# Where the split activations and weights begin within a partition: one offset mod 256 for all of them

## The chip, the cores and the metric

The kernel runs on one core of a Trainium2 chip. The metric is the device time of one execution in microseconds. The kernel before takes 2351.78 us, the median of 3 runs that lie between 2351.42 and 2352.85 us.

## What is computed

One inference step of a hybrid backbone, one layer, for 128 context tokens and 256 latent tokens (384 in all), with 2048 channels, in float32. Nearly all of the work is dense products of the 384 tokens with large weight matrices:

```python
mod = silu(cond) @ w_ada + b_ada                       # 2048 x 12288, two conditions
h   = rmsnorm(x) * (1 + sc1) + sh1
z   = h @ w_in + b_in                                  # 2048 x 11792
y_a, y_b, y_c = conv(z) @ w_a_out, pool(z) @ w_pool, mlstm(z) @ w_c_out
x   = x + g1 * rmsnorm((ga*y_a + gb*y_b + gc*y_c) @ w_out)   # 2048 x 2048
h2  = rmsnorm(x) * (1 + sc2) + sh2
u, g = split(h2 @ w_ffn_up)                            # 2048 x 11264
x   = x + g2 * rmsnorm((gelu(dwconv3(g)) * u) @ w_ffn_down)  # 5632 x 2048
```

The outputs are the new context and latent tokens and the final mLSTM states.

## The kernel before, in words

**Three products for one.** Every float32 operand of a large product is split into a high part, rounded to float32r, and a low part, the rest. `split` (line 163) makes them: ScalarE copies the source into the high tile (line 164), VectorE subtracts it from the source (line 165). `mm3` (line 172) then issues three float32r matmuls into one PSUM bank: high weight with high activation (line 173), high weight with low activation (line 174), low weight with high activation (line 175). The profile names them by output, then stationary and moving operand: `ps<-hx,whi` multiplies an activation tile `hx` with a weight tile `whi`.

**The stream.** The weights pass through a list of pieces (`run_stream`, line 183), each up to 128 x 1024 floats (512 KB). SyncE loads a piece into one of four `raw` tiles, `split` makes `whi` and `wlo` of it (three tiles of each), two pieces ahead of the matmuls that use it. While a piece is in use, functions of other work (`bgq`) are issued behind it. The order of pieces is fixed by the program. In the first stage there are separate tiles `eraw`, `ehi`, `elo` for `w_ada`.

**The stages.** In order of time: the modulation and the first tiles of `w_in` (to about 155 us of the span); the rest of the input projection with the mLSTM heads beside it (to about 560 us); the merge gates with the three branch projections (to about 1080 us); `w_out` (to about 1204 us); the second norm and `w_up` (to about 1970 us); the 88 pieces of `w_down` (to the end).

- In the input projection, merge gates and `w_out` stages, an `mm3` has a 128 x 128 block of weights as stationary operand and all 384 tokens of one `hx` tile as moving operand: 384 columns. A column tile of the output takes 16 `hx` tiles, `hx0` to `hx15`, 48 matmuls in all, in two pieces of 24.
- The branch projections (`ab_use`, `c_use`) do the same from the tiles `yah`/`yal` (convolution), `plh`/`pll` (pooling) and `hch`/`hcl` (mLSTM) in place of `hx`.
- In the `w_up` stage two more columns (the shift of the modulation, `H2`) hang on the tokens: 386 columns (`HW`, line 26).
- For the mLSTM values (`v_use`, line 887) and for `w_down` (`down_mm`, line 1509) the roles are exchanged: a 128-token slice of an `hx` tile is the stationary operand, the weights are the moving one, with 256 and 512 columns. In the down projection the activations are split into `hx0`, `hx1` and `hx2` in turn (`down_split`, line 1502), each used for 18 matmuls of one piece.

**Where the tiles lie.** Tiles of the three pools `cp`, `wp` and `hp` are placed one behind the other in each partition, from the left, each start rounded up to 32 bytes. Offsets here are byte offsets in the partition, taken mod 256, read from the built program. All tiles `raw`, `whi` and `wlo` are 4096 bytes long and begin at 96. The tile `hx0` begins at 96 too. An `hx` tile holds the high row and then the low row (`h_pair`, line 358). With 386 columns a row has 1544 bytes and a tile 3088, which is placed as 3104, so `hx1` begins at 128, `hx2` at 160, and so on by 32, round to 96 again at `hx8`; the low row of each begins 8 further on. With 384 columns in the down projection a row has 1536 bytes, and high and low row begin at the same offset. The branch tiles (`yah`, `yal`, `plh`, `pll`, `hch`, `hcl`), which lie behind `hx15`, all begin at 96. All slices that are taken of these tiles as matmul operands are whole multiples of 512 bytes apart, so an operand has the offset of its row. The tiles `eraw`, `ehi`, `elo` and the first stage's stationary operand `cs4` are placed from the right side and begin at 224.

So the two operands of a float32r matmul begin at the same offset in the products with `w_ada`, in the branch projections, for `hx0` in the down projection and for the high rows of `hx0` and `hx8` elsewhere, and at different ones in the rest.

Of the kernel before, what the change touches and what calls it, by code (L numbers as in the profile page):

```python
# [12 lines left out]
F32 = mybir.dt.float32  # L13
F32R = mybir.dt.float32r
# [5 lines left out]
P = 128  # L20
# [3 lines left out]
LAT = 256  # L24
NT = SEQ + LAT
HW = NT + 2
GRID_W = 64
ROWS = LAT // GRID_W
WA = 512
# [10 lines left out]

CBUF = HALF + (SEQ + HALF) + ROWS * (GRID_W + HALF)
CPOS = CBUF - 2 * HALF
CLAT0 = HALF + SEQ + HALF
CROW = GRID_W + HALF

# [47 lines left out]
def body(ctx: ExitStack, tc: tile.TileContext, i, o):  # L93
    nc = tc.nc
# [10 lines left out]
    cp = ctx.enter_context(tc.tile_pool(name="const", bufs=1, side="left"))  # L105
    wp = ctx.enter_context(tc.tile_pool(name="wp", bufs=1, side="left"))
    hp = ctx.enter_context(tc.tile_pool(name="hp", bufs=1, side="left"))
# [5 lines left out]
    def name(base):  # L113
        uid[0] += 1
        return f"{base}{uid[0]}"
# [14 lines left out]
    def tmp(tag="t", n=NT, bufs=4, dt=F32):  # L130
        return cp.tile([P, n], dt, name=name(tag), tag=tag, bufs=bufs)
# [15 lines left out]
    G2 = cp.tile([P, 2, KD], F32, name="G2")  # L147
    dp = ctx.enter_context(tc.tile_pool(name="dp", bufs=1, space=bass.MemoryType.DRAM))
    G2D = dp.tile([2, D], F32, name="G2D")

    act.dma_start(condT, i["condT"])
    act.dma_start(vec, i["vec"])
# [10 lines left out]
    def split(hi, lo, src):  # L163
        act.activation(hi, src, AF.Copy)  # L164
        dve.tensor_sub(lo, src, hi.bitcast(F32))  # L165
# [6 lines left out]
    def mm3(out, wh, wl, x, xl, first, last):  # L172
        pe.matmul(out, wh, x, start=first, stop=False, skip_group_check=True)  # L173
        pe.matmul(out, wh, xl, start=False, stop=False, skip_group_check=True)  # L174
        pe.matmul(out, wl, x, start=False, stop=last, skip_group_check=True)  # L175
# [177 lines left out]
    hx = [None] * KD  # L353
# [3 lines left out]

    def h_pair(tag, n):

        t = hp.tile([P, 2, n], F32R, name=name("hx"), tag=tag)  # L360
        pr = Two()
        pr.hi, pr.lo = t[:, 0], t[:, 1]
        return pr

    def make_h(k):

        st = {}

        def p1():
            st["t"] = tmp()  # L370
            dve.tensor_mul(st["t"], x1[:, k], R["r1"])

        def p2():
            t = st["t"]
            act.activation(t[:, :SEQ], t[:, :SEQ], AF.Identity, bias=H1[:, k, 0:1], scale=S1[:, k, 0:1])
            act.activation(t[:, SEQ:], t[:, SEQ:], AF.Identity, bias=H1[:, k, 1:2], scale=S1[:, k, 1:2])
            pr = h_pair(f"hx{k}", HW)
            pr.hi, pr.lo = pr.hi[:, :NT], pr.lo[:, :NT]
            act.activation(pr.hi, t, AF.Copy)
            hx[k] = pr  # L380

        def p3():
            dve.tensor_sub(hx[k].lo, st["t"], hx[k].hi.bitcast(F32))

        return p1, p2, p3
# [297 lines left out]
    def za_after(c):  # L683
        def f():
# [3 lines left out]
            dve.scalar_tensor_tensor(b[:, HALF : HALF + SEQ], ps[:, :SEQ], bias, s[:, :SEQ], ALU.add, ALU.mult)  # L688
            lat = b[:, CLAT0:].rearrange("p (r c) -> p r c", c=CROW)[:, :, :GRID_W]
            dve.scalar_tensor_tensor(lat, ps[:, SEQ:NT].rearrange("p (r c) -> p r c", c=GRID_W), bias,  # L690
                                     s[:, SEQ:].rearrange("p (r c) -> p r c", c=GRID_W), ALU.add, ALU.mult)
            glu["b", c] = b
# [514 lines left out]
    def scaled(out, src, G, k):  # L1207
        act.activation(out[:, :SEQ], src[:, :SEQ], AF.Copy, scale=G[:, k, 0:1])
        act.activation(out[:, SEQ:NT], src[:, SEQ:NT], AF.Copy, scale=G[:, k, 1:2])
# [19 lines left out]
    def split_mix(k):  # L1229
        pr = h_pair(f"hx{k}", HW)  # L1230
        split(pr.hi[:, :NT], pr.lo[:, :NT], mix[k])
        pr.hi, pr.lo = pr.hi[:, :NT], pr.lo[:, :NT]
        mixp[k] = pr
# [75 lines left out]
    def h2_b(k):  # L1309
        if k < KD:  # L1310
            x = X["x"][:, k]
            u = tmp("sig", HW, bufs=3)
            scaled(u, x, S2, k)
            act.activation(u[:, NT:], H2[:, k], AF.Copy)
            pr = h_pair(f"hx{k}", HW)
            act.activation(pr.hi, u, AF.Copy)  # L1316
            hx[k] = pr
            HU[k] = u
            if k == 0:
                act.activation(ss3, x, AF.Square)  # L1320
            else:
                HU["s", k] = tmp()
                act.activation(HU["s", k], x, AF.Square)
# [7 lines left out]
    def h2_step(k):  # L1331
        h2_a(k + 1)
        h2_b(k)
        h2_c(k)
# [20 lines left out]
    def up0_use(k):  # L1355
        def f(hi, lo):
            for c in range(NUP0):
                if k == 0:
                    acc["up", c] = accbank() if c < 2 else bank(2 + c)
                w = slice(c * P, (c + 1) * P)  # L1360
                mm3(acc["up", c][:, :HW], hi[:, w], lo[:, w], hx[k].hi, hx[k].lo, k == 0, k == KD - 1)
            h2_step(k + 2)
# [8 lines left out]
    def up_after(n):  # L1371
# [5 lines left out]
        def first():  # L1377
            pu, pg = acc[("up", 2 * n)], acc[("up", 2 * n + 1)]
            r = R["r3"]
            hb = tmp("hb", 4, bufs=2)  # L1380
            act.activation(hb[:, 0:2], pu[:, NT:HW], AF.Copy)
            act.activation(hb[:, 2:4], pg[:, NT:HW], AF.Copy)
# [100 lines left out]
    def g2_rows():  # L1483
# [4 lines left out]
        act.activation(row[0 : 2 * KD], ps[0 : 2 * KD, 0:P], AF.Copy)  # L1488
        gp.dma_start(G2D.rearrange("c (k p) -> (c k) p", p=P), row[0 : 2 * KD])
        g2_load(0)  # L1490

    def g2_load(h):
        t = F["p"].tile([P, 2, HALF_D], F32, name=name("gb"), tag="gb")
        for c in range(2):
            gp.dma_start(t[:, c], G2D[c : c + 1, HALF_D * h : HALF_D * (h + 1)].broadcast_to([P, HALF_D]))
        DN["g", h] = t
# [209 lines left out]
```

## Time and profile before

| | |
|---|---|
| time, median of 3 runs | 2351.78 us |
| time of the profiled execution | 2352.14 us |
| its span | 2350.4 us |
| granted TensorE clock, mean | 0.995 |
| PE busy | 2312.1 us (98%) |
| PEld busy | 2189.8 us (93%) |
| DVE busy | 1490.0 us (63%) |
| ACT busy | 933.8 us (40%) |
| chain of work that ended last, PE's share | 94% |

The span is the profiled execution from its first instruction to its last; the execution's own time is 1.7 us longer. PE is TensorE's matmuls, PEld its weight loads, DVE VectorE, ACT ScalarE, POOL GpSimd. Matmuls overlap: one begins before the one ahead has ended, so that the duration of one says less than the distance from its start to the next one's start, which is the time that a matmul takes of the stream. The text calls this distance the spacing. It is got from the timeline view, which gives every start to 0.01 us, as the time between two starts over the number of matmuls between them, or from the windows view as the length of a window that is full of matmuls over their number.

### The profile page before, as it was taken

To read this page: it belongs to the slowest core of one execution; us is meant where nothing else is said; L and a number is where in the kernel's file an instruction comes from. 1 tells how busy PE (TensorE), PEld (TensorE's weight loads), DVE (VectorE), ACT (ScalarE), POOL (GpSimd) and SP (SyncE) were. 2 spreads that over 40 slices of the span, in tenths; PEclk is the share of its full clock that TensorE was granted. 3 is DMA by queue.
4 is the path that set the end of the run, shared out by engine and by line. 5 is a ranking of instruction groups with operands and counts; after the bars stand their busy time and mean duration, and the time that the engine had idled before them with its cause. 6 is when DMAs were issued, how large, how long until landed. Compare 5 with 4: busy or idle time off the path is not lost.

```text
span 2350.4 us, 32026 instructions
## 1 busy us (share of the span) xinstructions
PE 2312.1 (98%) x12597; PEld 2189.8 (93%) x12597; DVE 1490.0 (63%) x2286; ACT 933.8 (40%) x1417; POOL 33.0 (1%) x72
## 2 busy tenths in 40 slices
PE   7999999999999999999999999999999999999997
PEld 3899999999999999999999999999999999888886
DVE  6876777646788777868556577776444445444444
ACT  6853333434322232324356533333333334334333
POOL 0000000000000000000000000000000000000000
PEclk9999999999999999999999999999999999999999
DMA  9954334234566666667533355554343333334332
GB/s 342 326 159 143 100 119 128 95 112 156 193 219 222 223 219 231 229 201 276 190 90 126 122 186 186 187 182 160 126 144 123 121 125 126 126 125 144 128 127 103
DMA packets 109335, 390.07 MB, mean 166 GB/s; under 512 B 12608, under 2 KB 12880, under 8 KB 109184
## 3 DMA queue, kind: packets, MB, share of 16 engines
q1 hardware_dynamic: 103968, 371.77, 47.6%
q0 software_dynamic: 4064, 14.36, 2.1%
q8 instruction: 98, 1.61, 0.3%
q10 hardware_dynamic: 1152, 1.90, 0.2%
q14 instruction: 53, 0.43, 0.1%
HBM read 382.71 MB, written 5.27 MB: 165 GB/s over the span
## 4 chain that ended last, share of the span: by engine, by line
PE 94%; DVE 2%; ACT 1%; DMA 1%; issue 1%; DVEq 0%; ACTq 0%; SPq 0%
PE ps L175 24%; PE ps L174 24%; PE ps L173 24%; PE ps L1513 5%; PE ps L1514 5%; PE ps L1512 5%; PE ps L897 1%; PE ps L899 1%; PE ps L898 1%; PE ps L400 1%; PE ps L994 1%; PE ps L989 1%; PE ps L401 1%; DMA eraw<-w_ada 0%; ACT ehi L164 0%
## 5 line engine op out<-in xcount | busy, mean ns | idle before, releaser
L165 DVE TENSOR_TENSOR wlo<-raw,whi 128x1024 fp32r<-128x1024 f32 (+2 forms) x520 | 622.5, 1199 | 755.0 <-ACT whi L164 754.8
L164 ACT ACTIVATE whi<-raw 128x1024 fp32r<-128x1024 f32 (+2 forms) x520 | 540.2, 1040 | 1272.3 <-PE ps L174 804.5
L173 PE MATMUL ps<-hx,whi 128*128 128x384 f32 (+1 forms) x3024 | 1026.7, 340 | 3.2 <-ACT hx L1316 3.2
L175 PE MATMUL ps<-hx,wlo 128*128 128x384 f32 (+1 forms) x3024 | 1026.6, 339 | 2.1 <-DVE wlo L165 2.1
L174 PE MATMUL ps<-hx,whi 128*128 128x384 f32 (+1 forms) x3024 | 1026.8, 340 | 0.1
L173 PEld LDWEIGHTS ps<-hx,whi 128*128 128x128 f32 x3024 | 571.5, 189 | 4.5 <-ACT hx L1316 3.4
L175 PEld LDWEIGHTS ps<-hx,wlo 128*128 128x128 f32 x3024 | 572.3, 189 | 3.5 <-DVE wlo L165 3.4
L174 PEld LDWEIGHTS ps<-hx,whi 128*128 128x128 f32 x3024 | 570.5, 189 | 1.8 <-DVE hx L165 0.4
L1177 DVE SCALAR_TENSOR_TENSOR cb<-raw,cb 128x1024 f32<-128x1024 f32 x256 | 313.1, 1223 | 9.2 <-DMA raw<-w_ada 3.3
L1513 PE MATMUL ps<-whi,hx 128*128 128x512 f32 x528 | 208.0, 394 | 0.8 <-DVE hx L165 0.8
L1514 PE MATMUL ps<-wlo,hx 128*128 128x512 f32 x528 | 208.2, 394 | 0.0
L1512 PE MATMUL ps<-whi,hx 128*128 128x512 f32 x528 | 207.8, 394 | 0.0
L1513 PEld LDWEIGHTS ps<-whi,hx 128*128 128x128 f32 x528 | 99.2, 188 | 24.4 <-DVE hx L165 1.1
L1512 PEld LDWEIGHTS ps<-whi,hx 128*128 128x128 f32 x528 | 99.2, 188 | 23.3 <-ACT hx L164 0.4
L1514 PEld LDWEIGHTS ps<-wlo,hx 128*128 128x128 f32 x528 | 99.2, 188 | 22.9
L165 DVE TENSOR_TENSOR elo<-eraw,ehi 128x1024 fp32r<-128x1024 f32 x56 | 66.9, 1221 | 22.8 <-ACT ehi L164 22.7
L712 DVE SCALAR_TENSOR_TENSOR cacc<-cbuf,vec,cacc 128x444 f32<-128x444 f32 x116 | 78.7, 679 | 2.8
L1404 DVE SCALAR_TENSOR_TENSOR t<-t,vec,t 128x192 f32<-128x192 f32 (+1 forms) x176 | 63.8, 383 | 16.1 <-ACT t L1395 12.9
L164 ACT ACTIVATE ehi<-eraw 128x1024 fp32r<-128x1024 f32 x56 | 56.3, 1047 | 18.8 <-DMA eraw<-w_ada 9.8
L897 PE MATMUL ps<-whi,hx 128*128 128x256 f32 x192 | 56.1, 292 | 0.0
L400 PE MATMUL ps<-ehi,cs 128*128 128x512 f32 x112 | 47.3, 422 | 6.9 <-ACT ehi L164 6.9
L898 PE MATMUL ps<-whi,hx 128*128 128x256 f32 x192 | 53.8, 280 | 0.0
(291 smaller groups left out, 1633.6 us busy)
## 6 DMA issues: line engine op xcount, KB each, us to landing
raw<-w_in SPq DMA_DIRECT2D x168, 512.0 KB, 3.9
raw<-w_up SPq DMA_DIRECT2D x164, 512.0 KB, 3.6
raw<-w_ada SPq DMA_DIRECT2D x128, 512.0 KB, 4.2
raw<-w_down SPq DMA_DIRECT2D x88, 512.0 KB, 3.2
eraw<-w_ada SPq DMA_DIRECT2D x64, 512.0 KB, 6.0
raw<-w_out SPq DMA_DIRECT2D x32, 512.0 KB, 4.6
raw<-w_v SPq DMA_DIRECT2D x16, 512.0 KB, 3.9
raw<-w_br SPq DMA_DIRECT2D x16, 512.0 KB, 4.9
```

Of the source, the lines that this page charges most:

```text
L164: act.activation(hi, src, AF.Copy)
L165: dve.tensor_sub(lo, src, hi.bitcast(F32))
L173: pe.matmul(out, wh, x, start=first, stop=False, skip_group_check=True)
L174: pe.matmul(out, wh, xl, start=False, stop=False, skip_group_check=True)
L175: pe.matmul(out, wl, x, start=False, stop=last, skip_group_check=True)
L712: dve.scalar_tensor_tensor(a, b[:, j : j + CPOS], w, a, ALU.mult, ALU.add)
L897: pe.matmul(outs[t], xh, hi[:, a], start=k == 0 and t != 1, stop=False, skip_group_check=True)
L898: pe.matmul(outs[t], xl, hi[:, a], start=False, stop=False, skip_group_check=True)
L1177: dve.scalar_tensor_tensor(MX["junk"], raw, 1.0, MX["cb"][c][half], ALU.mult, ALU.mult, accum_out=MODR[:, m, n, c, half : half + 1])
L1512: pe.matmul(ps, xh, hi[:, w], start=first, stop=False, skip_group_check=True)
L1513: pe.matmul(ps, xl, hi[:, w], start=False, stop=False, skip_group_check=True)
L1514: pe.matmul(ps, xh, lo[:, w], start=False, stop=last, skip_group_check=True)
```

## The change

The offsets are made equal, by four edits. An `hx` tile gets two rows of 448 floats (1792 bytes, 7 times 256), whatever the number of columns in use, so a tile has 3584 bytes (14 times 256) and both rows of all sixteen tiles begin at one offset. A tile `spare` of 128 bytes that nothing uses is put into the first pool, which moves all tiles behind it by 128: `raw`, `whi`, `wlo`, all `hx` rows and the branch tiles now begin at 224, where the tiles placed from the right side begin. The longer `hx` tiles need 7680 bytes more; for them the scratch area for the descriptors of GpSimd's DMAs, at the start of each partition, is halved from 16384 to 8192 bytes (itself a multiple of 256).

```diff
+HPITCH = 448
...
+    cp.tile([P, 32], F32, name="spare")
...
     def h_pair(tag, n):
 
-        t = hp.tile([P, 2, n], F32R, name=name("hx"), tag=tag)
+        t = hp.tile([P, 2, HPITCH], F32R, name=name("hx"), tag=tag)
         pr = Two()
-        pr.hi, pr.lo = t[:, 0], t[:, 1]
+        pr.hi, pr.lo = t[:, 0, :n], t[:, 1, :n]
         return pr
...
-    nc = bacc.Bacc("TRN2", target_bir_lowering=False, num_devices=1)
+    nc = bacc.Bacc("TRN2", target_bir_lowering=False, num_devices=1, dynamic_dma_scratch_size=8192)
```

The instructions of every engine and queue are the same as before in kind, shape and order; only addresses differ, and line numbers behind the first edits by 1 to 3.

## Rows read from the trace of the kernel before

**Rows 1.** The page: busy time of each engine; chain that ended last, by engine.
```profile
PE 2312.1 (98%) x12597; PEld 2189.8 (93%) x12597; DVE 1490.0 (63%) x2286; ACT 933.8 (40%) x1417; POOL 33.0 (1%) x72
PE 94%; DVE 2%; ACT 1%; DMA 1%; issue 1%; DVEq 0%; ACTq 0%; SPq 0%
```

**Rows 2.** Groups by line and form: count, busy us, mean ns, idle before.
```profile
L174 PE MATMUL ps<-hx,whi 128*128 128x384 f32 x1616 | 545.9, 338 | 0.1
...
L174 PE MATMUL ps<-hx,whi 128*128 128x386 f32 x1408 | 481.0, 342 | 0.0
...
L1513 PE MATMUL ps<-whi,hx 128*128 128x512 f32 x528 | 208.0, 394 | 0.8 <-DVE hx L165 0.8
...
L898 PE MATMUL ps<-whi,hx 128*128 128x256 f32 x192 | 53.8, 280 | 0.0
```

**Rows 3.** Waits, all engines: who for whom, us in total, times, longest.
```profile
ACT whi L164 <- PE ps L174: 804.5, 329, 5.7
...
PE ps L175 <- DVE wlo L165: 2.1, 4, 0.6
```

**Rows 4.** Windows, all instructions: the stages, PE count in brackets, clock, DMA share.
```profile
0.00:155.00 155.00, 136.68 (x610) 102.37 (x611) 109.06 (x147) 106.19 (x150) 7.24 (x15) 0.98 0.83 296
...
155.00:560.00 405.00, 404.04 (x2444) 388.50 (x2443) 273.52 (x513) 154.78 (x234) 16.83 (x40) 1.00 0.37 116
560.00:1080.00 520.00, 518.98 (x2957) 518.01 (x2956) 405.68 (x582) 169.36 (x205) 6.30 (x12) 1.00 0.66 219
1080.00:1195.00 115.00, 115.00 (x655) 115.00 (x654) 72.48 (x96) 41.68 (x66) 0.00 (x0) 1.00 0.60 202
```

**Rows 5.** Windows, instructions on `hx` tiles alone: first stage, up projection, down projection.
```profile
0.00:155.00 155.00, 52.11 (x288) 50.54 (x289) 8.76 (x16) 8.42 (x16) 0.98 0.83 296
...
1400.00:1900.00 500.00, 500.00 (x2818) 499.84 (x2818) 0.00 (x0) 0.00 (x0) 1.00 0.47 153
2050.00:2300.00 250.00, 250.00 (x1081) 202.77 (x1080) 33.15 (x60) 30.46 (x60) 1.00 0.40 130
```

**Rows 6.** Timeline of PE, a branch projection: start us, duration us, instruction.
```profile
580.12 0.33 PE L173 MATMUL ps<-yah,whi 128*128 128x384 f32 x1
...
580.82 0.35 PE L174 MATMUL ps<-yal,whi 128*128 128x384 f32 x1
...
582.22 0.33 PE L173 MATMUL ps<-plh,whi 128*128 128x384 f32 x1
...
582.74 0.33 PE L173 MATMUL ps<-hch,whi 128*128 128x384 f32 x1
...
586.90 0.33 PE L173 MATMUL ps<-hx,whi 128*128 128x384 f32 x1
```

**Rows 7.** Durations, ns, min/median/max: `hch` matmuls; line 174, 1400 to 1900 us.
```profile
L173 PE MATMUL ps<-hch,whi x128: 334/334/334, 582.7 to 1067.8; 128*128 128x384 f32 x128
...
L174 PE MATMUL ps<-hx,whi x939: 336/341/347, 1400.2 to 1899.8; 128*128 128x386 f32 x188
```

**Rows 8.** Timeline of PE, down projection: `hx2` from 2203.82, `hx0` from 2208.01, `hx1` from 2212.13.
```profile
2203.82 0.40 PE L1512 MATMUL ps<-whi,hx 128*128 128x512 f32 x1
...
2208.01 0.39 PE L1512 MATMUL ps<-whi,hx 128*128 128x512 f32 x1
...
2209.86 0.39 PE L1514 MATMUL ps<-wlo,hx 128*128 128x512 f32 x1
...
2211.90 0.40 PE L1514 MATMUL ps<-wlo,hx 128*128 128x512 f32 x1
2212.13 0.39 PE L1512 MATMUL ps<-whi,hx 128*128 128x512 f32 x1
```

**Rows 9.** Timeline of PE, mLSTM values, two rows 51 matmuls apart.
```profile
185.92 0.28 PE L897 MATMUL ps<-whi,hx 128*128 128x256 f32 x1
...
191.92 0.28 PE L897 MATMUL ps<-whi,hx 128*128 128x256 f32 x1
```

**Rows 10.** GpSimd's own load: the tokens for the second norm, issue, first use, landing.
```profile
L1297 DVE TENSOR_TENSOR x<-mo,x x16: 557/558/560, 1209.3 to 1253.9; 128x384 f32<-128x384 f32 x16
...
L1222 POOL DMA_DIRECT2D x<-xT x4: 527/528/530, 1064.6 to 1066.2; - x4
...
DMA to landing us min/median/max: 7.1/9.7/13.6
```

## The prediction

> **What bounds the kernel now.** First the page's busy times and its chain: PE is busy for 98% of the span and has 94% of the chain that ended last [rows 1]. Next the waits, to see whether something else sets PE's pace. They run the other way: ScalarE waited 804.5 us in all for PE to give weight tiles back, and PE's matmuls of line 175 waited 2.1 us for VectorE's low part [rows 3]. The granted clock is 1.00 in every stage from 155 us on, so 2.4 GHz [rows 4]. So from 155 us to the end the time is the number of matmuls times their spacing, and a change that only moves addresses can only act through that spacing, or not at all. In the first 155 us PE is not full (136.68 us, 610 matmuls, DMA share 0.83) [rows 4].
>
> So the question for the trace is whether the spacing depends on where operands begin. It does. The matmuls on `hch` have equal offsets for both operands. From the first of them at 582.74 us to the first `hx` matmul at 586.90 us there are 24: 4.16 us, **173.3 ns** each [rows 6]. In the `w_out` stage the same shape comes from `hx` tiles at eight offsets: 655 matmuls in 115.00 us, **175.6 ns** [rows 4]. The durations say the same: 334 ns for all 128 `hch` matmuls of a line, without any spread, and 336 to 347 ns among the `hx` matmuls of 386 columns [rows 7]. The down projection is the cleanest case, since there only the offset of the tile differs from one piece to the next: the 18 matmuls on `hx2` take 4.19 us (2203.82 to 2208.01), 232.8 ns each; the 18 on `hx0`, where the offsets are equal, 4.12 us (to 2212.13), 228.9 ns; and within these, once it has settled, 9 matmuls take 2.04 us (2209.86 to 2211.90), **226.7 ns** [rows 8]. It takes some matmuls to settle: the 12 on `yah`/`yal`, equal in offset but behind a run of unequal ones, take 2.10 us (580.12 to 582.22), 175.0 ns each, one of them 0.35 us long, and then the 3 on `plh` run at 173.3 [rows 6].
>
> I read this as two streams of reads, the moving operand and the next weights, that get in each other's way for a few ns per matmul unless they run in step, and as a state in step that a run of equal offsets finds and keeps. The change puts all of the stream into it.
>
> **A rule against it.** The Trainium skill, TensorE: Matmul & The Clock Gate, "Step-by-step: what each phase is for", says that PE has two independent SBUF read ports, so that "Loading the next tile's weights doesn't steal SBUF read bandwidth from the running matmul." By that rule offsets would not matter and the change would give nothing; the rows above, 228.9 against 232.8 ns for one shape in neighbouring pieces, do not agree with it. It stays as a rival below.
>
> **The terms.** No instruction is added, removed or moved on any engine or queue. What is left is the spacing, form by form, with counts from the groups (three lines per form) [rows 2].
>
> - *384 columns on `hx`.* 3 x 1616 = 4848, of which 288 lie in the first 155 us [rows 5], where PE has slack; I count 4560. They go from 175.6 to 173.3: 4560 x 2.3 ns = 10.5 us. The branch projections are in step already; only the settling of `yah` goes, 192 matmuls x 1.7 ns = 0.3 us.
> - *386 columns.* 3 x 1408 = 4224. Now 2818 matmuls take 500.00 us, 177.4 ns [rows 5]. No row shows this form in step. Between 384 and 512 columns the spacing in step grows by 53.4 ns for 128 columns, 0.417 ns a column, so two columns more would give 173.3 + 0.8 = 174.1. That is one end, and the value I take, because the same slope holds between two forms that were seen and the start of both reads is what the state in step seems to hang on. 4224 x 3.3 ns = 13.9 us. The other end is above today's spacing: a row of 1544 bytes does not end on a multiple of 256, unlike 1536 and 2048, so the step could be lost at each row's end. A duration is 334 - 173.3 = 161 ns longer than its spacing, so the longest seen in this stage, 347 ns [rows 7], is a spacing of 186: 4224 x 8.6 = 36 us of loss.
> - *512 columns.* 3 x 528 = 1584, now 1081 in 250.00 us, 231.3 ns [rows 5], in step 226.7: 1584 x 4.6 = 7.3 us.
> - *256 columns.* 3 x 192 = 576, now 51 in 6.00 us, 117.6 ns [rows 9]. By the slope in step it would be 226.7 - 256 x 0.417 = 119.9, so here being in step costs: 576 x 2.3 = 1.3 us. The other end is no change.
> - *What is behind PE.* With 1.3% less time for PE, every split must be 1.3% sooner. VectorE is busy 405.68 of 520 us in the merge stage and the DMA share is 0.66 [rows 4], so both stay below PE. In the input projection the head work comes in bursts, and some weights will be later than PE wants them; I give back 1 us. At nothing I take the splits themselves (ScalarE and VectorE read and write the same tiles at equal offsets before and after) and the halved scratch area: of GpSimd's DMAs the ones with a due time are the tokens for the second norm, issued from 1064.6 us, landed within 13.6, and first used at 1209.3 [rows 10]. If that cover of 130 us were not enough, PE would wait at 1209 us.
>
> Sum: 10.5 + 0.3 + 13.9 + 7.3 - 1.3 - 1.0 = 29.7 us. Against the profiled execution's 2352.1 us that is 2322.4; the median of the runs is 0.3 lower, so I forecast **2322 us** (1.3% faster). A measurement of this kernel can tell about 0.2% (4.7 us) from no change.
>
> **The rivals.**
>
> 1. *386 columns find no step.* The state in step holds for rows that are multiples of 256 bytes and not for 1544. For it: no aligned run of 386 columns was ever seen. Against it: with unequal offsets the 386 form stands above the 384 form by only 177.4 - 175.6 = 1.8 ns, so its odd end seems to cost little. The term of 13.9 us falls away: 2336 us, and up to 2347 if the spacing rises to 180.
> 2. *386 columns collide each time (slower).* Equal starts with rows that end 8 bytes past a multiple of 256 might bring the two reads together at the same place in every matmul, where unequal ones spread it. Place: the `w_up` stage, 1211 to 1970 us. It decides from the spacing at which it eats the other terms, 15.8 us / 4224 = 3.7 ns above today's 177.4, so from 181.1 ns on; at 186, 36.3 us of loss against 15.8 of gain, 2372 us. Such a spacing is among those seen [rows 7], but as the worst of a mixture whose mean is 177.4.
> 3. *The offsets do nothing.* The 173.3 ns of `hch` comes from something else about the branch tiles (high and low rows lie far apart there), and the two reads never meet: 2352 us. Against it stands `hx0` beside `hx1` and `hx2`, which are alike but for their offset [rows 8]. The rule of the Trainium skill named above (TensorE: Matmul & The Clock Gate) speaks for this rival.
> 4. *The gain is lost in waits.* PE's shorter pieces run into late splits or loads in the input projection and merge stages, so only the up and down projections gain: 13.9 + 7.3 = 21 us, 2331; if it holds everywhere, 2340 or more. Against it: 804.5 us of ScalarE waiting for PE [rows 3].
>
> **How the numbers follow.** The forecast 0.72; rival 1, 0.13; rival 2, 0.05; rival 3, 0.05; rival 4, 0.05. The forecast's own range is 2317 (nothing lost at 256 columns or in waits, and some `hx` runs better still) to 2330 (386 columns at 176, a bit of waiting). With most of rivals 1 and 4 the range is 2316 to 2340. Faster by over 0.2%: the forecast, rival 1 and most of rival 4, 0.89; within 0.2%: rival 3, 0.05; slower: rival 2 with a little for mishaps, 0.06.
>
> **What the profile after should show.** Durations of 334 ns without spread for 384-column matmuls on `hx`, as on `hch` now, and near 388 for 512 columns. In the windows, 1400 to 1900 us: about 2870 matmuls if 386 columns run at 174.1, 2818 or fewer if rival 1 or 2 holds. In the down projection pieces of 18 matmuls that all take 4.08 us, whichever `hx` tile. The counts of instructions unchanged. The prediction is wrong if `hx` matmuls of 384 columns keep a spread of durations; the theory stands but its size is off if only the 386-column stage does.

## The result: 19.3 us faster, and the profile after

The changed kernel takes 2332.68 us (median of 4 executions, 2331.24 to 2332.71) beside 2351.97 us before (median of 4, 2351.42 to 2352.85). The ratio is 0.9916, 95% interval 0.9904 to 0.9928: 19.3 us less. The forecast was 2322 us. The profiled execution shown here took 2332.71 us, with a span of 2330.9 us.

The page, first the busy times of the engines, then the chain of work that ended last (compare [rows 1]):

```profile
PE 2292.1 (98%) x12597; PEld 2177.4 (93%) x12597; DVE 1490.2 (64%) x2286; ACT 934.0 (40%) x1417; POOL 33.1 (1%) x72
...
PE 94%; DVE 2%; DMA 2%; ACT 1%; issue 1%; DVEq 0%; ACTq 0%; SPq 0%
```

PE still bounds the kernel, with the same counts of instructions; it is busy for 20.0 us less, which covers the whole change. The groups by form (line, engine, form and count, then busy us, mean ns, idle before) answer to [rows 2]; all line numbers are larger by 3. In these names the moving operand stands first and the stationary one second, and not the other way round as was said ahead of the prediction: `hx,whi` are 384 or 386 columns of activations that move, with a block of weights stationary, and `whi,hx` is the reverse.

```profile
L177 PE MATMUL ps<-hx,whi 128*128 128x384 f32 x1616 | 540.2, 334 | 0.2 <-DVE hx L168 0.2
...
L177 PE MATMUL ps<-hx,whi 128*128 128x386 f32 x1408 | 477.9, 339 | 0.0
...
L1516 PE MATMUL ps<-whi,hx 128*128 128x512 f32 x528 | 205.5, 389 | 0.8 <-DVE hx L168 0.8
...
L901 PE MATMUL ps<-whi,hx 128*128 128x256 f32 x192 | 54.3, 283 | 0.0
```

The mean duration of the 384-column matmuls fell from 338 to 334 ns and that of the 512-column ones from 394 to 389; the 386-column ones fell by only 3 ns, from 342 to 339, and stand 5 ns above the 384-column ones for two columns more. The durations of single forms (min/median/max in ns, with the first and the last start) say more than their means:

```profile
L177 PE MATMUL ps<-hx,whi x944: 338/339/342, 1400.0 to 1899.9; 128*128 128x386 f32 x189
...
L1516 PE MATMUL ps<-whi,hx x368: 389/389/389, 2049.9 to 2299.5; 128*128 128x512 f32 x184
```

In `w_out`, line 177 has 334/334/334 ns, as the `hch` matmuls had before [rows 7]. The down projection has lost its spread too. The up projection has kept one. The windows, of instructions on `hx` tiles alone (columns: length; busy us with count of PE, PEld, DVE, ACT; granted clock, DMA share, GB/s), answer to [rows 5]:

```profile
1400.00:1900.00 500.00, 500.00 (x2831) 499.84 (x2830) 0.00 (x0) 0.00 (x0) 1.00 0.46 153
2050.00:2300.00 250.00, 250.00 (x1105) 207.01 (x1104) 34.14 (x62) 30.87 (x61) 1.00 0.40 131
```

2831 matmuls of 386 columns in 500 us are 176.6 ns each (before, 177.4); 1105 of 512 columns in 250 us are 226.2 (before, 231.3). A window also counts the matmuls that are cut by its ends, so these run 0.1 to 0.5 ns low. From here on "mean spacing" is the mean of all distances from one matmul's start to the next one's in a stage, without the gaps; the records give starts to 1 ns. The timeline of PE (start us, duration us, instruction) shows three places: the start of the up projection, its middle, and one piece of the down projection.

```profile
1201.96 0.69 PE L176 MATMUL ps<-hx,whi 128*128 128x386 f32 x1 [3.24 <-ACT hx L1319]
...
1203.05 0.53 PE L178 MATMUL ps<-hx,wlo 128*128 128x386 f32 x1
...
1207.87 0.36 PE L178 MATMUL ps<-hx,wlo 128*128 128x386 f32 x1
...
1499.95 0.34 PE L176 MATMUL ps<-hx,whi 128*128 128x386 f32 x1
1500.13 0.34 PE L177 MATMUL ps<-hx,whi 128*128 128x386 f32 x1
1500.30 0.34 PE L178 MATMUL ps<-hx,wlo 128*128 128x386 f32 x1
1500.48 0.34 PE L176 MATMUL ps<-hx,whi 128*128 128x386 f32 x1
...
2208.11 0.39 PE L1515 MATMUL ps<-whi,hx 128*128 128x512 f32 x1
...
2212.18 0.39 PE L1515 MATMUL ps<-whi,hx 128*128 128x512 f32 x1
```

The 18 matmuls of the piece at 2208.11 take 4.07 us; before, they took 4.12 on `hx0` and 4.19 on `hx2` [rows 8]. In the middle of the up projection the starts do not come evenly: by the records, spacings of 175 and 178 ns alternate.

Where the 19.4 us between the two spans come from, by the first matmul of each stage in the two traces:

| stage | gained there, us | gained up to its end, us |
|---|---|---|
| first stage and first part of the input projection, to the mLSTM values | 0.8 | 0.8 |
| rest of the input projection | 1.5 | 2.3 |
| merge gates and branch projections | 5.6 | 7.9 |
| `w_out` and the second norm | 1.6 | 9.5 |
| up projection | 2.4 | 11.9 |
| down projection | 7.7 | 19.6 |

The end of the kernel behind the last of these matmuls gives about 0.15 us back.

### The profile page after: what moved, and what is told of

It is laid out like the page before. It is cut to its first block, busy times and chain, and to the rows that moved or that the text cites. A ratio compares the mean times of both kernels' runs of the same rounds, so it can differ in the third digit from the quotient of the medians.

```text
span 2330.9 us, 32026 instructions
## 1 busy us (share of the span) xinstructions
PE 2292.1 (98%) x12597; PEld 2177.4 (93%) x12597; DVE 1490.2 (64%) x2286; ACT 934.0 (40%) x1417; POOL 33.1 (1%) x72
## 4 chain that ended last, share of the span: by engine, by line
PE 94%; DVE 2%; DMA 2%; ACT 1%; issue 1%; DVEq 0%; ACTq 0%; SPq 0%
PE ps L177 24%; PE ps L178 24%; PE ps L176 24%; PE ps L1516 5%; PE ps L1515 5%; PE ps L1517 5%; DMA eraw<-w_ada 1%; PE ps L901 1%; PE ps L902 1%; PE ps L900 1%; PE ps L997 1%; PE ps L992 1%; PE ps L403 0%; DVE wlo L168 0%; PE ps L404 0%
## 5 line engine op out<-in xcount | busy, mean ns | idle before, releaser
L167 ACT ACTIVATE whi<-raw 128x1024 fp32r<-128x1024 f32 (+2 forms) x520 | 540.3, 1040 | 1252.7 <-PE ps L177 773.6
L1516 PE MATMUL ps<-whi,hx 128*128 128x512 f32 x528 | 205.5, 389 | 0.8 <-DVE hx L168 0.8
L1515 PE MATMUL ps<-whi,hx 128*128 128x512 f32 x528 | 205.5, 389 | 0.0
L902 PE MATMUL ps<-wlo,hx 128*128 128x256 f32 x192 | 54.3, 283 | 0.0
```

The source lines that it names most:

```text
L1515: pe.matmul(ps, xh, hi[:, w], start=first, stop=False, skip_group_check=True)
L1516: pe.matmul(ps, xl, hi[:, w], start=False, stop=False, skip_group_check=True)
```

## The experiments

"Distance" is the offset of an activation row less that of the weights it meets, mod 256. The kernel before ran beside the experiments at 2352.67 us (median of 7; `no_spare`, `up392`, `up384`, `mixed`), 2351.9 (one execution; the two sweeps, `lo_plus128`, `widths`) and 2351.09 (median of 9; the other four). All diffs are against the changed kernel. Unless said otherwise, the rows are from the windows view on `hx` tiles, with the columns given above: `w_out` (1085 to 1190 us), the up projection (1400 to 1900), the down projection (2050 to 2300). The changed kernel itself has 605 or so matmuls in the first of these stretches (173.3 ns each).

### `no_spare`: everything at 96 in place of 224

```diff
-    cp.tile([P, 32], F32, name="spare")
```

> The changed kernel without the spare tile: weights, hx rows and branch tiles all begin at 96 instead of 224; the tiles placed from the right stay at 224. If only the two operands' offsets relative to each other matter, nothing changes: 173.3 ns at 384 columns, 226.7 at 512, 2332.7 us within 1.5. If the offset itself matters (or that of the weights against the tiles on the right), the spacing goes back towards 175.6 and 231.3 and the time towards 2350.

2331.80 us (2 executions; ratio to before 0.9912, 0.9892 to 0.9931).

```profile
1400.00:1900.00 500.00, 500.00 (x2831) 499.83 (x2831) 0.00 (x0) 0.00 (x0) 1.00 0.46 153
2050.00:2300.00 250.00, 250.00 (x1105) 207.07 (x1104) 33.81 (x62) 30.87 (x61) 1.00 0.39 131
```

The counts are those of the changed kernel, and the mean spacings too: 173.46, 176.66 and 226.71 ns for 384, 386 and 512 columns. So it makes no difference whether both operands begin at 96 or at 224. One of the four edits does nothing.

### `up384`: the two odd columns taken away

The product of the two modulation columns with `w_ffn_up` is left out.

```diff
-                mm3(acc["up", t][:, :HW], hi[:, a], lo[:, a], hx[k].hi, hx[k].lo, k == 0, k == KD - 1)
+                mm3(acc["up", t][:, :NT], hi[:, a], lo[:, a], hx[k].hi[:, :NT], hx[k].lo[:, :NT], k == 0, k == KD - 1)
```

> The changed kernel with 384 columns in the up projection. It leaves out the product of the shift H2 with w_ffn_up (the first two tokens' columns are put in its place). If the whole of the missing gain sits in the two odd columns, the stage runs at 173.3 ns like every other 384-column stage: 4224 x 3.3 ns = 14 us less than the changed kernel, 2319 us, which with the 3.5 us that two columns were priced at in the prediction is the forecast's 2322. If something else in this stage (its vector work, its weights' loads) holds the spacing up, it stays above 175 ns and the time above 2326 us.

2317.64 us (2 executions; 0.9851, 0.9832 to 0.9871).

```profile
1400.00:1900.00 500.00, 500.00 (x2886) 499.84 (x2885) 0.00 (x0) 0.00 (x0) 1.00 0.46 154
```

55 matmuls more fit into the 500 us, and the mean spacing is 173.4 ns, as elsewhere at 384 columns. The two columns cost 2332.7 - 2317.6 = 15.0 us. So the stage itself, its loads and its other engines, does not hold the up projection back: at these offsets its width does.

### `up392`: 392 columns, a row of 1568 bytes

The six further columns repeat the modulation ones and are not used.

```diff
-HW = NT + 2
+HW = NT + 8
```

> The changed kernel with 392 columns in place of 386 in the up projection: the two columns of the shift stand there four times over. Question: what keeps the 386-column form from the step. Theory A (the stream is read in units of 8 columns, 32 bytes, so 386 columns cost as much as 392): the spacing stays at 176.7 ns, even from matmul to matmul instead of 175 and 178 in turn, and the time stays within 2 us of the changed kernel's 2332.7. Theory B (a row that does not end on a multiple of 256 bytes loses the step at its end, and each column counts): spacing 176.7 + 6 x 0.417 = 179.2 ns or more, 4224 x 2.5 ns = 10.6 us longer, 2343 us. Theory C (units of 16 columns or 64 bytes, averaged over two matmuls): (400 + 32) cycles at 2.4 GHz, 180 ns, 2347 us.

2334.80 us (2 executions; 0.9924, 0.9904 to 0.9944).

```profile
1400.00:1900.00 500.00, 500.00 (x2821) 499.83 (x2820) 0.00 (x0) 0.00 (x0) 1.00 0.46 152
```

The mean spacing is 177.34 ns in a cycle of five: 180, 178, 177, 180, 172. None of the expected values was met. That a row ends on a multiple of 32 bytes is not enough for even spacing, and six more columns cost only 0.7 ns.

### `widths`: six widths by turns

In the up projection every tile of the output takes one of six widths by turns; the columns past 386 are copies that nobody reads.

```diff
+WIDTHS = (386, 388, 392, 400, 416, 448)
...
+                n = WIDTHS[t % 6]
+                mm3(acc["up", t][:, :n], hi[:, a], lo[:, a], hx[k].hi[:, :n], hx[k].lo[:, :n], k == 0, k == KD - 1)
```

> The changed kernel with the column tiles of the up projection run 386, 388, 392, 400, 416 and 448 columns wide in turn (the columns past 386 hold copies and are not used). It asks which row lengths keep the step, that is, a spacing without spread that is the columns plus 32 at 2.4 GHz. Theory R (a row of whole 256 bytes): only 448 columns, at 200.0 ns; 416 and 400 spread and lie above 186.7 and 180.0. Theory R64 (whole 64 bytes): 400 at 180.0, 416 at 186.7 and 448 at 200.0, all without spread; 386, 388 and 392 with spread, up to 3 ns above columns plus 32 (174.2, 175.0, 176.7). Theory A (whole 32 bytes, rounded up), already strained by the 392-column run's 177.3: 176.7 for 386, 388 and 392, and 180.0, 186.7, 200.0.

2358.54 us (one execution), with more columns to compute. The timeline of PE, the first matmul of each tile of 48:

```profile
1446.48 0.34 PE L177 MATMUL ps<-hx,whi 128*128 128x400 f32 x1
...
1455.13 0.35 PE L177 MATMUL ps<-hx,whi 128*128 128x416 f32 x1
...
1464.16 0.37 PE L177 MATMUL ps<-hx,whi 128*128 128x448 f32 x1
...
1473.90 0.34 PE L177 MATMUL ps<-hx,whi 128*128 128x386 f32 x1
...
1482.38 0.34 PE L177 MATMUL ps<-hx,whi 128*128 128x388 f32 x1
...
1490.85 0.34 PE L177 MATMUL ps<-hx,whi 128*128 128x392 f32 x1
...
1499.37 0.34 PE L177 MATMUL ps<-hx,whi 128*128 128x400 f32 x1
```

From one start to the next, over 48: 400 columns 180.2 ns, 416 188.1, 448 202.9, 386 176.7, 388 176.5, 392 177.5. Over all tiles, once settled, the mean spacings and the most frequent cycles by the records are:

| columns | bytes of a row | mean ns | cycle ns | (columns + 32) at 2.4 GHz, ns |
|---|---|---|---|---|
| 384 (changed kernel) | 1536 | 173.3 | even | 173.3 |
| 386 | 1544 | 176.7 | 175, 178 | 174.2 |
| 388 | 1552 | 176.7 | 182, 172 | 175.0 |
| 392 | 1568 | 177.3 | five | 176.7 |
| 400 | 1600 | 180.0 | even | 180.0 |
| 416 | 1664 | 188.3 | 190, 183, 191, 189 | 186.7 |
| 448 | 1792 | 203.4 | five: 202, 199, 207, 202, 203 | 200.0 |
| 512 (changed kernel) | 2048 | 226.7 | even | 226.7 |

The last column is only arithmetic that fits the cases called even. Two widths have more than one cycle in this trace. One tile of 416 columns out of thirteen (from 1349 us) runs evenly at 186.7 ns, the others at 188.3. Two tiles of 448 out of thirteen (from 1358 and 1729 us) run evenly at 206.7 ns and the others at 202.8, so that the 203.4 is a mixture. 448 columns have a row of seven times 256 bytes and do not run at 200.0; 400 have not and are even at 180.0 in every tile. So "a row that ends on a multiple of 256 bytes" is not what decides, nor is a multiple of 64.

### `sweep_a` and `sweep_b`: one constant distance in each stage

In `sweep_a` both rows of an `hx` tile stand at distance 128 in the input projection and merge gates, 64 in `w_out` and 128 in the up projection; in `sweep_b` at 32, 192 and 64. In the down projection the distance changes from piece to piece, by 32 in `sweep_a` and by 8 in `sweep_b`.

```diff
-    def h_pair(tag, n):
+    def h_pair(tag, n, o=0):
...
-        pr.hi, pr.lo = t[:, 0, :n], t[:, 1, :n]
+        pr.hi, pr.lo = t[:, 0, o : o + n], t[:, 1, o : o + n]
...
+            pr = h_pair(f"hx{k}", NT, 32)
...
+        pr = h_pair(f"hx{k}", NT, 16)
...
+            pr = h_pair(f"hx{k}", HW, 32)
...
+        pr = h_pair(f"hx{s % 3}", NT, 8 * (s % 8))
```

(The numbers are floats of 4 bytes; `sweep_b` has 8, 48, 16 and `2 * (s % 8)`.)

> The changed kernel, with the hx rows begun a fixed distance behind the weights' offset: +128 bytes in the input projection, merge gates and up projection, +64 in the w_out stage, and in the down projection 0, 32, 64, ... 224 from piece to piece. The branch tiles stay at equal offsets. Theory E (equality mod 256 makes the step): all hx stages lose it, 384 columns at 175.5 ns or more, and in the down projection only every eighth piece comes near 226.7 ns, the other seven lie at 231 to 235. Theory C (any constant distance does, only the change from tile to tile hurt before): 173.3 and 226.7 ns everywhere. Theory H (equality mod 128 is enough): 173.3 at +128, and in the down projection two of eight pieces, 0 and 128, at 226.7; the w_out stage at 175.5 or more.

> The same with other distances: +32 bytes in the input projection and merge gates, +192 in the w_out stage, +64 in the up projection, and 0, 8, 16, ... 56 from piece to piece in the down projection. Theory E: only the pieces at 0 come near 226.7 ns, all else lies at 231 to 235 there and at 175.5 or more at 384 columns. Theory C: 173.3 and 226.7 everywhere. A third way, theory L (the reads meet by lines of 32 bytes): pieces at 0, 8, 16 and 24 are alike and near 226.7, those at 32 to 56 are not.

2349.14 and 2333.85 us (one execution each). `sweep_a`:

```profile
1085.00:1190.00 105.00, 105.00 (x608) 105.00 (x607) 0.00 (x0) 0.00 (x0) 1.00 0.60 200
1400.00:1900.00 500.00, 500.00 (x2832) 499.84 (x2831) 0.00 (x0) 0.00 (x0) 1.00 0.46 154
2050.00:2300.00 250.00, 250.00 (x1078) 202.31 (x1077) 33.10 (x60) 30.49 (x60) 1.00 0.38 130
```

`sweep_b`:

```profile
1085.00:1190.00 105.00, 105.00 (x607) 105.00 (x607) 0.00 (x0) 0.00 (x0) 1.00 0.57 188
1400.00:1900.00 500.00, 500.00 (x2859) 499.84 (x2858) 0.00 (x0) 0.00 (x0) 1.00 0.45 153
2050.00:2300.00 250.00, 250.00 (x1080) 202.89 (x1079) 32.90 (x60) 30.55 (x60) 1.00 0.37 129
```

No theory put down beforehand (E, C, H, L) fits both runs as a whole. At 384 columns the operands need not begin at one offset: distances 32, 64 and 192 give 173.9, 173.3 and 173.4 ns in the mean. At 32 this mean is one of different levels and not of a stream that settles: between two interruptions by other matmuls the stream keeps one cycle to the end, and of the 32 such stretches in the input projection 19 run at 173.3 (the 95 matmuls from 302.8 us: 175, 172) and 13 at about 176.6 (the 95 from 385.3 us: 175, 180, 174, 178); in the merge gates all run at 173.3. At 192 the long stretch of `w_out` runs at 173.3 and the short last one (23 matmuls, to 1195 us) at 176.8. In the changed kernel every stretch of these stages, 50 in all, comes to the even 173.3 within seven matmuls. Distance 128 was not seen at 173.3: 176.0 ns, in a cycle of five (175, 182, 175, 174, 174), while the `hch` matmuls of the same execution run at 173.3. At 386 columns a distance of 128 gives 176.67, the same mean as equal offsets but in a cycle of four, and 64 gives 175.0.

At 512 columns equality does count, within pieces of 18 matmuls. The timeline of PE in `sweep_a`, the first matmul of four neighbouring pieces of 18; the piece from 2200.43 is the one at distance 0:

```profile
2196.22 0.40 PE L1513 MATMUL ps<-whi,hx 128*128 128x512 f32 x1
...
2200.43 0.40 PE L1513 MATMUL ps<-whi,hx 128*128 128x512 f32 x1
...
2204.55 0.39 PE L1513 MATMUL ps<-whi,hx 128*128 128x512 f32 x1
...
2208.74 0.40 PE L1513 MATMUL ps<-whi,hx 128*128 128x512 f32 x1
```

4.21, 4.12 and 4.19 us. In the second half of a piece (its 9th to 17th spacing), all pieces of a distance together, the mean is 226.7 ns at 0; 233.5, 233.6, 233.9, 231.7, 233.3, 228.9 and 233.3 at 32, 64 and so on to 224; and 230.6, 233.5, 230.1, 233.1, 233.2 and 233.3 at 8, 16, 24, 40, 48 and 56. Of fourteen distances only 0 gives the even 226.7. Each piece follows one at another distance, so what a longer stream at one such distance would come to was not tried.

### `lo_plus128`: high rows equal, low rows 128 bytes on, in all stages

```diff
-        pr.hi, pr.lo = t[:, 0, :n], t[:, 1, :n]
+        pr.hi, pr.lo = t[:, 0, 0:0 + n], t[:, 1, 32:32 + n]
```

> The changed kernel with only the low hx rows begun 128 bytes further on; high rows and both weights stay equal. It asks which two reads meet: of the three matmuls of a product only the middle one streams the low row, and the weights for the third are loaded meanwhile. If the step needs each matmul's stream and the weights loaded beside it at one offset, the mean over the three goes up to 175 or more at 384 columns and the time to 2340 or more. If the stream is compared with nothing but the matmul's own weights or the step holds over one matmul in three, 384 columns stay within 0.5 ns of 173.3 and the time within 4 us of 2332.7.

2345.85 us (one execution).

```profile
1085.00:1190.00 105.00, 105.00 (x600) 105.00 (x599) 0.00 (x0) 0.00 (x0) 1.00 0.58 194
```

Here the distance goes 0, 128, 0 within each three matmuls. At 384 columns the mean is 175.55 ns, in a cycle of six (176, 179, 174, 181, 170, 174): two thirds of the matmuls have equal offsets, and nearly all of the gain at 384 columns is gone. Two at 173.3 and one at 176.0 (distance 128 in `sweep_a`) would be 174.2 in the mean, so the change of distance itself costs too.

### `step_tiles` and `lo_plus8`: the two halves of the change

Before, two things differed from equal offsets at 384 and 386 columns: each `hx` tile began 32 bytes after the one ahead, and its low row 8 bytes after its high row. `step_tiles` brings back the first alone, `lo_plus8` the second alone, both outside the down projection, which stays as changed.

```diff
-            pr = h_pair(f"hx{k}", HW)
+            pr = h_pair(f"hx{k}", HW, 8 * (k % 8), 8 * (k % 8))
```

```diff
-            pr = h_pair(f"hx{k}", HW)
+            pr = h_pair(f"hx{k}", HW, 0, 2)
```

(`h_pair` takes the start of the high and of the low row in floats; each edit stands in three places.)

> One part of the change undone: the hx rows of every stage but the down projection step on by 32 bytes from tile to tile, as before the change, while high and low row of a tile begin at the same offset. Theory S (a distance that changes between matmuls costs, whichever it is): 384 columns go back to 175.2 ns or more, the time to 2340 or more. Theory Q (the low row's 8 bytes past the high row did the harm, being less than a line of 32): 384 columns stay at 173.3 to 173.9, the time under 2337.

> The other part undone: all hx tiles begin at the weights' offset, but the low row 8 bytes further on, as before the change (not in the down projection). Theory S: 384 columns go back to 175.2 ns or more, 2340 us or more, since the distance changes twice in each product. Theory Q: the same or worse, and the whole of the loss. If 8 bytes are too little to matter: 173.3 to 173.9 and under 2337 us, and the step from tile to tile did it all.

2339.43 and 2324.59 us (one execution each). `step_tiles`:

```profile
1085.00:1190.00 105.00, 105.00 (x601) 105.00 (x600) 0.00 (x0) 0.00 (x0) 1.00 0.58 192
1400.00:1900.00 500.00, 500.00 (x2831) 499.84 (x2830) 0.00 (x0) 0.00 (x0) 1.00 0.46 154
```

`lo_plus8`:

```profile
1085.00:1190.00 105.00, 105.00 (x600) 105.00 (x599) 0.00 (x0) 0.00 (x0) 1.00 0.56 187
1400.00:1900.00 500.00, 500.00 (x2886) 499.84 (x2885) 0.00 (x0) 0.00 (x0) 1.00 0.46 155
```

Mean spacings, ns:

| | 384 columns | 386 columns |
|---|---|---|
| before: tiles step, low row 8 on | 175.7 | 177.5 |
| `step_tiles`: tiles step, rows equal | 175.25 | 176.7 |
| `lo_plus8`: tiles equal, low row 8 on | 174.81 | 173.51 |
| changed kernel: both equal | 173.46 | 176.66 |

At 384 columns both halves of the change are needed. At 386 columns the tiles' half alone takes off 4.0 ns in this execution, more than the 3.3 of the prediction, and making the rows equal as well loses 3.15 of them again; no expectation had this. With a worse time at 384 columns, `lo_plus8` is still 8.1 us faster than the changed kernel and the fastest here that computes everything.

The 173.51 is not the only level of this kernel, though. Its timeline, 48 matmuls before and 48 behind the place where others (lines 313 and 322) come in between:

```profile
1250.61 0.33 PE L176 MATMUL ps<-hx,whi 128*128 128x386 f32 x1
...
1259.04 0.33 PE L176 MATMUL ps<-hx,whi 128*128 128x386 f32 x1
...
1267.41 0.34 PE L176 MATMUL ps<-hx,whi 128*128 128x386 f32 x1
...
1275.73 0.34 PE L176 MATMUL ps<-hx,whi 128*128 128x386 f32 x1
```

8.43 us before, 175.6 ns each (cycle 175, 181, 171); 8.32 us behind, 173.3 ns each (174, 171, 175), and so to the end of the stage. Had it stayed at 175.6, an estimate by 4224 x 2.05 ns is 8.7 us more, 2333 us, as slow as the changed kernel. At 384 columns it has two levels as well, 174.4 and 175.6 ns, both above 173.3.

### `up64`, `mixed` and `mixed64`: other ways for the two columns

`up64` moves both rows to distance 64 in the up projection alone. `mixed` takes the low part of the two modulation columns as two more columns of the high row, so that the three matmuls of an `mm3` have 388, 384 and 386 columns; `mixed64` does both.

```diff
-            pr = h_pair(f"hx{k}", HW)
+            pr = h_pair(f"hx{k}", HW, 16, 16)
```

```diff
+    def mm3u(out, wh, wl, x, xl, first, last):
+        pe.matmul(out[:, : HW + 2], wh, x, start=first, stop=False, skip_group_check=True)
+        pe.matmul(out[:, :NT], wh, xl[:, :NT], start=False, stop=False, skip_group_check=True)
+        pe.matmul(out[:, :HW], wl, x[:, :HW], start=False, stop=last, skip_group_check=True)
...
+            dve.tensor_sub(hx[k].hi[:, HW:], HU[k][:, NT:], hx[k].hi[:, NT:HW].bitcast(F32))
```

> The changed kernel with the hx rows of the up projection alone begun 64 bytes behind the weights' offset. With that distance 386 columns ran at 175.0 ns in an earlier run, against 176.7 at equal offsets; input projection, merge gates, w_out and down projection keep equal offsets. If the spacing depends on width and distance in the stage alone: 4224 x 1.66 = 7.0 us less than the changed kernel, 2325.7 us. If the 175.0 hung on something else of that run, 2332.7.

> The changed kernel with the same sums done in rows of 388, 384 and 386 columns: the low part of the shift stands behind its high part in the high row, so that the product with the low row needs no extra columns. If a spacing in step is the columns rounded up to 8, plus 32, at 2.4 GHz, and the step survives rows of different length, the three take 176.7, 173.3 and 176.7 ns, 175.6 in the mean against 176.7: 4224 x 1.1 = 4.7 us less than the changed kernel, 2328 us. If rows of different length break the step, the mean is 177.5 or more, as with unequal offsets, and the time 2336 us or more.

> Rows of 388, 384 and 386 columns as in the earlier run (2327.8 us, mean spacing 175.5), now also 64 bytes behind the weights' offset. If the gains of width and distance add, the mean goes to (2 x 175.0 + 173.3) / 3 = 174.4 ns, 4224 x 1.1 = 4.6 us less, 2323 us. If they do not, because each mixture of widths finds a cycle of its own, the mean lies anywhere between 174.4 and 177.5 and the time between 2323 and 2336.

| | median us | executions | ratio to before | matmuls in 1400 to 1900 us | cycle in the up projection, ns |
|---|---|---|---|---|---|
| `up64` | 2331.21 | 5: 2325.85 to 2333.78 | 0.9906 (0.9892 to 0.9919) | 2833 | partly 182, 176, 175 |
| `mixed` | 2327.78 | 4: 2326.92 to 2329.12 | 0.9894 (0.9878 to 0.9911) | 2850 | 178.4, 172.6, 176 |
| `mixed64` | 2337.24 | 5: 2335.72 to 2338.32 | 0.9938 (0.9926 to 0.9951) | 2813 | 183.5, 176, 174 |

`mixed` met its time, but not by the spacings that were added up for it: its 384-column matmul starts the next one sooner than any even stream of 384 does, and its 388-column one later. `mixed64` met neither of its sums in time; its row in the windows view, 500 us for fewer matmuls than even before the change [rows 5]:

```profile
1400.00:1900.00 500.00, 500.00 (x2813) 499.84 (x2813) 0.00 (x0) 0.00 (x0) 1.00 0.45 152
```

Its trace has three levels one behind the other: 173.3 ns for the first 258 matmuls that run without a break (from 1215 us), better than the 174.4 of gains that add; then 175.6 for 287; then 177.8 to the end.

`up64` stands at 64, where `sweep_b` had 175.0 ns. Two of its five executions (2325.85 and 2326.33 us) come near the 2325.7 us that follow from that; the others (2331.21, 2331.55 and 2333.78) do not. The profiled one, of 2331.21 us, shows another cycle for part of the stage (182, 176, 175, mean 177.8), 176.4 in all, and its timeline shows where it begins, at twelve transposes of line 1476:

```profile
1302.32 0.34 PE L177 MATMUL ps<-hx,whi 128*128 128x386 f32 x1
...
1310.72 0.34 PE L177 MATMUL ps<-hx,whi 128*128 128x386 f32 x1
...
1311.59 1.47 PE L1476 MATMUL ps<-ident,x 128*128 128x128 f32 x12
...
1313.08 0.34 PE L177 MATMUL ps<-hx,whi 128*128 128x386 f32 x1
...
1321.08 0.34 PE L177 MATMUL ps<-hx,whi 128*128 128x386 f32 x1
```

48 matmuls before it take 8.40 us, 175.0 ns each; 45 behind it 8.00 us, 177.8 ns each. The stream keeps this level through three more such interruptions, until a transpose of line 1489 at 1692.30 us, and then runs at 175.0 to the end. Some 2104 matmuls at 177.8 in place of 175.0 are 5.8 us; without them the execution would have taken 2325.4 us by this estimate, like the two short ones. So one program at one distance has more than one level. In these traces a stream keeps its cycle as long as nothing comes in between, and every change of level in `up64`, `mixed64` and `lo_plus8` sits at such an interruption; most interruptions change nothing, and what picks the level behind one was not found. The changed kernel came back to 176.7 after each of its six in this stage.

## Why the prediction was right and where it was wrong

**What bounds the kernel, and the sign: right.** The counts are unchanged, PE's share of the chain is 94% as before, and the gain lies in the spacing. The time is inside the range of 2316 to 2340, but only because that was widened for rivals 1 and 4: it is outside the forecast's own 2317 to 2330, 10.7 us above the forecast and nearest to rival 1.

**384 columns, 10.5 us: right.** By the starts the mean spacing fell from 175.7 to 173.46 ns (the 175.6 that the prediction counted in a window of `w_out` is 176.1 there), and 4560 x 2.24 ns = 10.2 us. Settling behind `yah` is gone as well (175.1 to 173.3). Against this stand the 256-column matmuls: from 117.8 to 119.7 ns, 576 x 1.9 = 1.1 us of loss, where 1.3 was forecast. Together that is 9.4 us, and the stages up to `w_out` gained 9.5. The sum was right, though the reason was half right: at this width a stream can also run at 173.3 ns at a constant distance of 32, 64 or 192, though at 32 and 192 not always.

**512 columns, 7.3 us: right.** Spacing 231.6 to 226.7 ns, 1584 x 4.9 = 7.8 us; the down projection gained 7.7. Here equality is what counts, as far as pieces of 18 show it.

**Waits, 1.0 us: right in size by luck, at another place.** ScalarE's wait for PE fell only from 804.5 to 773.6 us [rows 3], so splits did not become late. What was given back lies at the start of the up projection. PE waits 3.24 us for the first `hx` there in both traces, and then begins at the lower granted clock, 0.51 in the kernel before (1211.42 to 1215.06 us) and 0.50 in the changed one (1201.96 to 1207.87). In the kernel before:

```profile
1211.42 0.69 PE L173 MATMUL ps<-hx,whi 128*128 128x386 f32 x1 [3.24 <-ACT hx L1316]
...
1214.76 0.47 PE L173 MATMUL ps<-hx,whi 128*128 128x386 f32 x1
1215.06 0.34 PE L174 MATMUL ps<-hx,whi 128*128 128x386 f32 x1
```

Before, ten matmuls came 0.3 us or more apart (1211.42 to 1215.06), which is the 1.2 GHz level; after, seventeen did (1201.96 to 1207.87, shown above). Seven of them at 0.32 in place of 0.18 us are 1.0 us. At the 193rd matmul of the stage 0.9 us had been given back. The wait itself had not grown, so the halved scratch area and the load of tokens [rows 10] cost nothing here; why the lower clock lasted longer is open.

**386 columns, 13.9 us: wrong, and this is the whole miss.** The step that failed is the one from "between 384 and 512 columns the spacing in step grows by 0.417 ns a column" to 174.1 ns. It took two even cases and drew a line between them, as if every width had an even state at equal offsets. Measured at equal offsets: 176.66 ns, so that 4224 x (177.49 - 176.66) = 3.5 us are left, less the 0.9 at the lower clock: 2.6, and the stage gained 2.4. With 174.1 the changed kernel would be 4224 x 2.56 = 10.8 us faster, 2321.9 us, which is the forecast.

Rival 1 named this outcome (386 columns find no step, 2336 us) and deserved more than 0.13. The argument against it was that the odd end adds only 1.8 ns when offsets are unequal, and that says nothing of equal ones. Its own reason, that the state holds only for rows of a multiple of 256 bytes, falls as well: 448 columns have such rows and run at 202.8 or 206.7 ns, never at the 200.0 of the arithmetic, and 400 do not and are even. Nor is the 174.1 out of reach at this width: `lo_plus8` has 173.51.

**Rivals 2 to 4** fell. At equal offsets the 386-column spacing did not rise above that of before; offsets do act; and the gain was not lost in waits. Rival 3 had the rule of the Trainium skill behind it that the weights' loading takes nothing from a running matmul's reads (TensorE: Matmul & The Clock Gate, "Step-by-step: what each phase is for"). In `sweep_a` neighbouring pieces that differ in their offset alone take 4.12 and 4.19 us, and the measurement decides against the rival; whether it is the loading of weights that the moving reads meet, no run here shows.

**What stays open.** That the moving operand's reads and those of the weights get in each other's way is argued from the dependence on their distance; which two reads meet, and whether the weights in question are the matmul's own or the next one's, was not separated, since `whi` and `wlo` always had one offset. The writes of ScalarE and VectorE into the same tiles, which move with the offsets, were not set apart either. Nor is there a rule that gives the cycle from width and distance. Equal offsets at 384 and 512 columns with the low row 8 bytes on in the up projection alone were not tried; by the spacings measured, an estimate is 2332.7 - 4224 x (176.66 - 173.51) = 2319 us, with the reserve that this takes the better of two levels that `lo_plus8` showed within its one execution.

## What to carry to other kernels

When PE is the bound, take the distance from one matmul's start to the next, form by form, and look for forms of one shape that differ in it: a few ns between them can hang on nothing but the operands' byte offsets mod 256. Keep the distance between moving and stationary operands the same along a stream (unpadded tiles and rows shift it unnoticed), start from equal offsets (at 384, 386 and 512 columns they came back to one level after every interruption here; at 416 and 448 they did not), and then try a few distances for each width, because a width that was not measured can't be had from its neighbours. Look at the spacing stretch by stretch, between the places where other matmuls come in, before a mean is compared, and execute more than once: a time from one execution may be one of several levels.

## What the runs showed that was not expected

- A stream of matmuls falls into a repeating cycle: of one to seven spacings at a constant distance, of twelve at 386 columns in `lo_plus128`, and of 24 in the kernel before and in `step_tiles`, where the distances themselves repeat after eight tiles. Of the eight widths in the table only 384, 400 and 512 columns became even at equal offsets in every tile or piece.
- The mean over such a cycle can be lower than the even spacing would be: in `lo_plus8` 173.3 ns at 386 columns from 1267 us on, the same as at 384.
- The same program on the same chip took 2325.85 and 2333.78 us. The one execution of it with a trace changed its cycle twice, each time where other matmuls came in between.
- After the same wait of 3.24 us PE ran ten matmuls at the lower clock in one trace and seventeen in the other.
